# First group's q projected second and its attention begun then, with gate and compressed branch among its steps, in a hybrid retention and sparse-attention layer

## The chip, the core and the metric

The kernel runs on one core of a Trainium2 chip. The metric is device time in microseconds (us), as the median of several runs. The profile is one further execution, recorded by the hardware profiler; its span runs from the first to the last recorded instruction, and its own time is that of the same execution.

In what follows PE is TensorE's matmul, PEld its loading of weights, DVE is VectorE, ACT is ScalarE, POOL is GpSimd, and SP is SyncE, on whose queue all DMAs of this kernel are issued.

## What is computed

One layer on `x` of 512 tokens by 1024. After an RMSNorm, one projection gives everything: q, k, v and gate of a retention group (8 heads of 64), and q, gate, three pairs of k and v (compressed, selected, window; 2 kv heads of 64 each) and branch gates of a sparse-attention group. Cut to its core:

```python
h = rms_norm(x, norm_w)
rq, rk, rv, rg, nq, ng, ck, cv, sk, sv, wk, wv, gl = split(h @ w_in)
o_ret = rms_norm(retention(rq, rk, rv), ret_norm_w)        # rope on rq, rk; decay, causal
y_ret = o_ret * silu(rg)
q  = rms_norm(nq, q_norm_w)
kc = rms_norm(silu((blocks(ck) + pos_k) @ w1_k) @ w2_k, k_norm_cmp)   # blocks of 32, stride 16
vc = silu((blocks(cv) + pos_v) @ w1_v) @ w2_v
o_cmp, p_cmp = softmax_attention(q, kc, vc)
o_slc = attention over the blocks of 64 with the highest p_cmp, k = rms_norm(sk, k_norm_slc)
o_win = causal window attention, k = rms_norm(wk, k_norm_win)
y_nsa = (g0 * o_cmp + g1 * o_slc + g2 * o_win) * silu(ng)   # g = sigmoid(gl + b_gate)
out = x + concat(y_ret, y_nsa) @ w_out
```

In what the kernel's names say, NQ is the projection of the attention's q, NG of its gate, SK of selected and window k and v, CK of compressed k and v; a 0 or 1 behind them is the kv group (four query heads each). RQ, RK, RV, RG are the retention's.

## The kernel before, in words

Every product of two fp32 matrices is done as three products of fp32r halves: `wh` is the rounded copy of a weight tile, `wl` the rest, and likewise `hTh` and `hTl` for the activations; high by high, high by low and low by high are summed in PSUM. Weights come in units of 512 KB (`raw`, two buffers). ACT makes `wh` from a unit (two casts of 128x512), and `wl = raw - wh` is subtracted by DVE or by POOL; a string such as "VPVP" in `add_units` says which of them takes which unit's half, and some are left for the planner to choose (`either`).

There are two ways to project. `proj` keeps the activations in the array (128 tokens) and moves 256 columns of weights, so that the result has tokens on partitions; its instructions read `psacc<-wh,hTl` with 128x256. `proj_f` keeps the weights in the array and moves all 512 tokens, so that the result is transposed (columns on partitions); they read `psacc<-hTh,wh` with 128x512. Accumulation in PSUM uses the tag "acc" (3 banks), scores "S" (2), transposes "T" (2), outputs "O" (1).

The program is recorded in one order, stage by stage: NG0, CK, the gather of the compression's input (`compress_in`), SK and NQ0 are "drained" (recorded entirely), and then attention begins. Each step of an attention tile is a generator: `stage_a` makes scores (`psS`), the mask (DVE), row maximum (`mx`, DVE) and exponential (`P`, ACT); `stage_b` scales `P`, transposes it (four 128x128 `psT`), splits it in `PTh` (ACT) and `PTl` (DVE) and multiplies by v (`psO`). Between the steps `fill(FILL_A[g] * c)` takes so many ns of projection pieces from a list of "fillers". The retention's pairs of heads (`ret_pair`) run in the same way, with `FILL_R`; the result of a pair goes through a norm on DVE and POOL (`oS`, `ss`, `rs`, `yr`), and is transposed on PE (`y_transpose`, `psT<-identr,yr`) for the output product. That product is cut in `out1` (three of four units, plus the residual) and `out2` (the fourth unit).

The recorded operations are then ordered by a list scheduler (`arrange`): it has a table of costs by engine and shape, looks at the first 48 ready operations of each engine in the order of the record, and writes out the order of all five engines. `FIRST` moves three kinds of operations ahead in that order (weight halves, evacuations of "acc", loads of `raw`). So all instructions carry the line number of the loop that emits them, L1274, and are known by the names of their tiles. A queue of finished attention tiles (`pend`, with the tile `ot`) waits for the gate and is worked off by POOL (`fin_tile`).

Keys and queries are stored twice on partitions: `stack` copies a split tile `HL` into `B` with three DMAs of SP per half (64x512 and 64x1024).

Of the kernel before, what the change touches and what calls it, by code (L numbers as in the profile page):

```python
# [16 lines left out]
P = 128  # L17
T = 512
# [9 lines left out]
FILL_A = (1100.0, 1500.0)  # L28
FILL_R = (1200.0, 1500.0)
# [44 lines left out]
def footprint(ap):  # L74
# [4 lines left out]
    p0, base = divmod(int(ap.offset), row)  # L79
    starts, run = [base], 1  # L80
    for s, n in sorted(dims[1:], key=lambda d: abs(d[0])):
        if n == 1 or s == 0:
            continue
        if abs(s) <= max(run, 8):
            run += abs(s) * (n - 1)
        else:
            starts = [b + s * i for b in starts for i in range(n)]
# [4 lines left out]
    return ap.tensor.name, p0, p0 + dims[0][1], bits  # L92
# [253 lines left out]
def rope_tables():  # L346

    half = HD // 2
# [5 lines left out]
    tab = np.stack([np.concatenate([cos, cos, cos, cos], 0), np.concatenate([-sin, sin, -sin, sin], 0)], 1)  # L354
# [4 lines left out]
def layer_kernel(ctx: ExitStack, tc: tile.TileContext, x, xt, norm_w, w_in, w_out, ret_w, rowp, colp,  # L359
# [7 lines left out]
    SBB = {"B": 8, "P": 2, "raw": 2, "wh": 4, "wl": 4, "HL": 2, "qn": 2, "sq": 3, "oS": 1, "ot": 2, "kn": 2,  # L367
# [42 lines left out]
    wv = w_in.rearrange("(k p) c -> p k c", p=P)  # L410
    add_units(w_in, NG, (0, 1), "VPVP")
    add_units(w_in, CK, (0, 1), "VPVP")
    add_units(w_in, SK, (0, 1), "VPVP")
    add_units(w_in, NQ, (0, 1), "VVVP")
# [128 lines left out]
    w2t = S([P, 2, 2, 64], "w2t")  # L543
# [43 lines left out]
    def proj_f(evac):  # L587

        banks = [None, None]
        for u in range(4):  # L590
            wh, wl = next_unit()
            for c in range(2):
                if u == 0:
                    banks[c] = PS("acc")
                for kk in range(2):
                    k = 2 * u + kk
                    wc = slice(c * P, c * P + P)
                    mm(banks[c], wh[:, kk, wc], hTh[:, k], k == 0, False)
                    mm(banks[c], wh[:, kk, wc], hTl[:, k], False, False)
                    mm(banks[c], wl[:, kk, wc], hTh[:, k], False, k == KT - 1)  # L600
                if u == 3:
# [51 lines left out]

    ckv = S([P, NT, 256], "yr")

    def ck_evac(b, bank):
        for t in range(2):
            A.activation(ckv[:, 2 * b + t], bank[:, 256 * t:256 * t + 256], AF.Copy, scale=sc(rs1, 2 * b + t))
# [75 lines left out]

    kcT = S([P, 2, 64], "kcT", F32R)
# [5 lines left out]
    def compress_in(kv):  # L741
        tp = PS("T")
        for t in range(NT):
            PE.transpose(tp[:, t * 128:t * 128 + 128], ckv[:, t, kv * 128:kv * 128 + 128], ident)
        kv2 = S([P, 2, 256], "sq")
        tv = tp.rearrange("p (m r) -> p r m", r=2)
# [565 lines left out]
```

## Time and profile before

| what | value |
|---|---|
| runs | 340.67, 341.05, 341.1 us (median 341.05) |
| profiled execution, its own time | 340.4 us |
| its span | 338.6 us, so 1.8 us lie around it |
| granted TensorE clock over the span | 0.998 of full speed |
| PE busy | 329.6 us, 97% of the span, 2229 matmuls |
| PEld busy | 296.0 us, 87% |
| DVE, ACT, POOL busy | 248.5 (73%), 213.0 (63%), 124.3 us (37%) |

Busy time counts an engine from the start to the end of each instruction, and a matmul's modelled end overlaps the next one's start, so a row's mean duration of a matmul is longer than the spacing of matmuls in a run. The spacing is read from the chain of waits, where a run of matmuls stands as start, length and count.

### The profile page before, as it was taken

The page shows a single profiled execution, that of the slowest core. Times are in us where ns is not written, and L with a number is a line of the kernel's source. Part 1 is how long each engine was busy: PE and PEld are TensorE (multiplying, and loading weights), DVE is VectorE, ACT ScalarE, POOL GpSimd, SP SyncE. Part 2 cuts the span into 40 slices and gives each one's busy share as a digit, 9 for nine tenths or more (in the row PEclk, how much of TensorE's full clock was granted, in tenths as well). Part 3 has the DMA queues.
Part 4 walks back from the last instruction along what each step waited for, and adds up shares of the span by engine and source line. Part 5 has one row for each costly group of instructions (what it writes and reads, how often), then busy time and mean ns, then how long its engine had stood idle before and what let it go on. Part 6 is the DMA issues. An engine that isn't in the chain of part 4 may idle for free.

```text
span 338.6 us, 6267 instructions
## 1 busy us (share of the span) xinstructions
PE 329.6 (97%) x2229; PEld 296.0 (87%) x2229; DVE 248.5 (73%) x481; ACT 213.0 (63%) x474; POOL 124.3 (37%) x110
## 2 busy tenths in 40 slices
PE   8999999999999999999999999999999998999996
PEld 5988999978899787879999899787879997999995
DVE  2847667467878986668788978867777888786663
ACT  5874384355889878497885588778855553444210
POOL 1025206130232613468149535406184474130300
PEclk9999999999999999999999999999999999999999
DMA  7985562598434427331955612223635677021224
GB/s 235 390 289 162 133 179 68 156 216 234 146 116 128 124 62 180 107 95 34 255 143 157 150 36 64 63 62 96 155 101 149 153 204 234 2 94 33 95 73 175
DMA packets 40366, 46.96 MB, mean 139 GB/s; under 512 B 3984, under 2 KB 34320, under 8 KB 40336
## 3 DMA queue, kind: packets, MB, share of 16 engines
q1 hardware_dynamic: 40336, 46.58, 48.5%
q8 instruction: 17, 0.28, 0.3%
q14 instruction: 13, 0.11, 0.1%
HBM read 31.89 MB, written 2.10 MB: 100 GB/s over the span
## 4 chain that ended last, share of the span: by engine, by line
PE 73%; DVE 8%; DMA 7%; ACT 5%; issue 3%; POOL 2%; SPq 2%; DVEq 0%; ACTq 0%; POOLq 0%
PE psacc L1274 48%; PE psT L1274 9%; PE psS L1274 9%; PE psO L1274 6%; DMA B<-HL 4%; DVE wl L1274 2%; SPq L1274 2%; DMA xw<-qn 2%; ACT P L1274 2%; DMA B<-xt 1%; ACT wh L1274 1%; DVE mx L1274 1%; DVE sq L1274 1%; DVE psS L1274 1%; DVE PTl L1274 1%
## 5 line engine op out<-in xcount | busy, mean ns | idle before, releaser
L1274 PE MATMUL psacc<-wh,hTl 128*128 128x256 f32 x384 | 97.1, 284 | 0.0
L1274 ACT CAST wh<-raw 128x512 fp32r<-128x512 f32 x88 | 53.3, 622 | 42.3 <-PE psacc L1274 33.0
L1274 PE MATMUL psacc<-wl,hTh 128*128 128x256 f32 x256 | 73.5, 288 | 0.2 <-DVE wl L1274 0.2
L1274 PE MATMUL psacc<-wh,hTh 128*128 128x256 f32 x256 | 72.8, 286 | 0.0
L1274 PEld LDWEIGHTS psacc<-wh,hTl 128*128 128x128 f32 x384 | 68.5, 189 | 0.5
L1274 DVE TENSOR_TENSOR wl<-raw,wh 128x512 fp32r<-128x512 f32 x64 | 49.8, 788 | 19.3 <-ACT wh L1274 18.2
L1274 POOL TENSOR_TENSOR wl<-raw,wh 128x512 fp32r<-128x512 f32 x24 | 31.4, 1310 | 54.8 <-ACT wh L1274 36.1
L1274 PEld LDWEIGHTS psacc<-wl,hTh 128*128 128x128 f32 x256 | 48.4, 189 | 1.0 <-DVE wl L1274 0.4
L1274 PEld LDWEIGHTS psacc<-wh,hTh 128*128 128x128 f32 x256 | 48.1, 188 | 0.6 <-DVE sq L1274 0.2
L1274 PE MATMUL psS<-B,B 128*128 128x256 f32 (+3 forms) x176 | 42.5, 334 | 1.1 <-ACT P L1274 0.6
L1274 PE MATMUL psacc<-hTh,wh 128*128 128x512 f32 x96 | 39.0, 406 | 0.0
L1274 PE MATMUL psacc<-hTl,wh 128*128 128x512 f32 x96 | 38.6, 402 | 0.0
L1274 PE MATMUL psacc<-hTh,wl 128*128 128x512 f32 x96 | 38.4, 402 | 0.0
L1274 ACT ACTIVATE P<-psS,mx 128x128 f32<-128x128 f32 (+3 forms) x64 | 33.7, 531 | 3.6 <-DVE mx L1274 3.3
L1274 DVE TENSOR_TENSOR PTl<-psT,PTh 128x512 fp32r<-128x512 f32 x40 | 27.0, 687 | 9.4 <-ACT PTh L1274 9.1
L1274 PEld LDWEIGHTS psS<-B,B 128*128 128x128 f32 x176 | 28.1, 188 | 5.2 <-ACT P L1274 2.3
L1274 POOL TENSOR_TENSOR rs<-ss,mhalf 128x8 f32<-128x8 f32 (+2 forms) x14 | 17.9, 1282 | 36.9 <-DVE ss L1274 36.6
L1274 DVE TENSOR_TENSOR psS<-psS,cst 128x128 f32<-128x128 f32 (+2 forms) x68 | 23.1, 347 | 10.1 <-PE psS L1274 9.2
L1274 ACT CAST PTh<-psT 128x512 fp32r<-128x512 f32 x40 | 23.2, 589 | 9.7 <-PE psT L1274 9.0
L1274 DVE TENSOR_REDUCE mx<-psS 128x1 f32<-128x384 f32 (+3 forms) x44 | 28.2, 640 | 1.1
L1274 PE MATMUL psT<-identr,P 128*128 128x128 f32 x160 | 28.8, 275 | 0.1
L1274 ACT ACTIVATE P<-P,r 128x384 f32<-128x384 f32 (+3 forms) x53 | 26.5, 562 | 0.9 <-DVE r L1274 0.9
(187 smaller groups left out, 691.8 us busy)
## 6 DMA issues: line engine op xcount, KB each, us to landing
raw<-w_in SPq DMA_DIRECT2D x28, 512.0 KB, 3.7
B<-HL SPq DMA_DIRECT2D x56, 128.0 KB, 3.8
B<-HL SPq DMA_DIRECT2D x12, 256.0 KB, 4.4
B<-xt SPq DMA_DIRECT2D x8, 256.0 KB, 5.1
B<-x SPq DMA_DIRECT2D x4, 512.0 KB, 8.0
raw<-w1k SPq DMA_DIRECT2D x4, 512.0 KB, 4.8
raw<-w1v SPq DMA_DIRECT2D x4, 512.0 KB, 3.9
xw<-qn SPq DMA_DIRECT2D x32, 64.0 KB, 2.0
```

What stands on the lines that cost most here:

```text
L1274: fn(*args, **kw)
```

## The change

The order of the record becomes: NQ0, then SK, then attention of group 0 at once. NG0 and CK are no longer drained before it but are the first two fillers, ahead of the work that was the first filler before. CK, the output product (out1, out2 and the last piece) are projected by `proj_f`, 512 tokens wide, and the output is therefore written transposed (the residual is read from the transposed `xt`). The compressed k and v come out of CK's bank already transposed: one multiplication by a broadcast row of the norm's factors (`rsb`) puts them where the compression wants them, without the tile `ckv`, its four ACT evacuations, eight transposes on PE and the copies behind these. The columns of RQ and RK are interleaved on the host, so that swapping the rope's halves takes two DMAs of every second partition in place of four of 32 partitions. The tile `ot` has four buffers in place of two. Two factors of one half are moved from one scalar operation to another. The numbers in FILL_A, FILL_R and FIRST change.

In the listing of the program, PE's products 256 wide go from 1296 to 828, those 512 wide from 455 to 689, and those 128 wide from 268 to 260. POOL has 126 operations in place of 115, DVE 477 in place of 483, ACT 397 in place of 407, SP 178 in place of 195. Subtractions for `wl` are 33 on POOL and 55 on DVE, in place of 24 and 64.

```diff
-FILL_A = (1100.0, 1500.0)
-FILL_R = (1200.0, 1500.0)
+FILL_A = (1800.0, 1400.0)
+FILL_R = (1200.0, 400.0)
...
-    tab = np.stack([np.concatenate([cos, cos, cos, cos], 0), np.concatenate([-sin, sin, -sin, sin], 0)], 1)
+    tab = np.stack([np.stack([cos, cos], 1), np.stack([-sin, sin], 1)], 2).reshape(HD, 2, T)
+    tab = np.concatenate([tab, tab], 0)
...
-    SBB = {"B": 8, "P": 2, "raw": 2, "wh": 4, "wl": 4, "HL": 2, "qn": 2, "sq": 3, "oS": 1, "ot": 2, "kn": 2,
+    SBB = {"B": 8, "P": 2, "raw": 2, "wh": 4, "wl": 4, "HL": 2, "qn": 2, "sq": 3, "oS": 1, "ot": 4, "kn": 2,
...
+    add_units(w_in, NQ, (0, 1), "VVVP")
+    add_units(w_in, SK, (0, 1), "VPVP")
     add_units(w_in, NG, (0, 1), "VPVP")
     add_units(w_in, CK, (0, 1), "VPVP")
-    add_units(w_in, SK, (0, 1), "VPVP")
-    add_units(w_in, NQ, (0, 1), "VVVP")
...
-    w2t = S([P, 2, 2, 64], "w2t")
+    w2t = S([P, 2, 2, 64], "xw")
...
-    def proj_f(evac):
+    def part_f(o, c, u, wh, wl, lh, ll, first, last, ts=slice(0, T)):
+        for kk in range(2):
+            k = 2 * u + kk
+            wc = slice(c * P, c * P + P)
+            mm(o, wh[:, kk, wc], lh(k)[:, ts], first and kk == 0, False)
+            mm(o, wh[:, kk, wc], ll(k)[:, ts], False, False)
+            mm(o, wl[:, kk, wc], lh(k)[:, ts], False, last and kk == 1)
+
+    def proj_f(evac, lh=hh_, ll=hl_, us=(0, 1, 2, 3)):
 
         banks = [None, None]
-        for u in range(4):
+        for u in us:
             wh, wl = next_unit()
             for c in range(2):
-                if u == 0:
+                if u == us[0]:
                     banks[c] = PS("acc")
-                for kk in range(2):
-                    k = 2 * u + kk
-                    wc = slice(c * P, c * P + P)
-                    mm(banks[c], wh[:, kk, wc], hTh[:, k], k == 0, False)
-                    mm(banks[c], wh[:, kk, wc], hTl[:, k], False, False)
-                    mm(banks[c], wl[:, kk, wc], hTh[:, k], False, k == KT - 1)
-                if u == 3:
+                part_f(banks[c], c, u, wh, wl, lh, ll, u == us[0], u == us[-1])
+                if u == us[-1]:
                     evac(c, banks[c])
                 yield 1400
...
-    ckv = S([P, NT, 256], "yr")
-
-    def ck_evac(b, bank):
-        for t in range(2):
-            A.activation(ckv[:, 2 * b + t], bank[:, 256 * t:256 * t + 256], AF.Copy, scale=sc(rs1, 2 * b + t))
...
+    rsb = S([P, T], "rsb")
+    rbp = PS("T")
+    for i in range(NT):
+        PE.transpose(rbp[:, i * P:i * P + P], sc(rs1, i).to_broadcast([P, P]), ident)
+    A.copy(rsb, rbp)
...
-    def compress_in(kv):
-        tp = PS("T")
-        for t in range(NT):
-            PE.transpose(tp[:, t * 128:t * 128 + 128], ckv[:, t, kv * 128:kv * 128 + 128], ident)
+    def ck_evac(kv, bank):
+
         kv2 = S([P, 2, 256], "sq")
-        tv = tp.rearrange("p (m r) -> p r m", r=2)
+        bv, rv = (v.rearrange("p (m r) -> p r m", r=2) for v in (bank, rsb))
         for g in range(2):
             for r in range(2):
-                dst, src = kv2[r * 64:r * 64 + 64, g, :], tv[g * 64:g * 64 + 64, r, :]
-                if r == 0:
-                    A.copy(dst, src)
-                else:
-                    V.tensor_copy(dst, src)
+                rows = slice(64 * g, 64 * g + 64)
+                V.tensor_tensor(kv2[r * 64:r * 64 + 64, g, :], bv[rows, r, :], rv[rows, r, :], op=ALU.mult)
...
-            sqc = S([64, 64], "sqc")
+            sqc = S([64, 64], "sq")
...
-    V.tensor_scalar(gates, gates, 0.5, 0.5, op0=ALU.mult, op1=ALU.add)
+    V.tensor_scalar(gates, gates, 0.25, 0.25, op0=ALU.mult, op1=ALU.add)
...
-            A.activation(y, t, AF.Tanh)
+            A.activation(y, t, AF.Tanh, scale=0.5)
...
-            for a in range(4):
-                b = a ^ 1
-                SP.dma_start(xw[32 * a:32 * a + 32], xs_[32 * b:32 * b + 32])
+            for r in range(2):
+                SP.dma_start(xw[r:P:2], xs_[1 - r:P:2])
...
-            while len(pend) >= 2:
+            while len(pend) >= 4:
...
-    drain(proj_f(ng_evac(0)))
-    drain(proj(ck_evac))
-    drain(compress_inputs())
+    drain(proj(q_evac(0)))
     drain(proj(kv_evac(0)))
-    drain(proj(q_evac(0)))
-    fillers += [inter(proj_f(ng_evac(1)), cgen[0]), inter(proj(q_evac(1)), cgen[1]),
+    fillers += [proj_f(ng_evac(0)), proj_f(ck_evac), inter(proj_f(ng_evac(1)), cgen[0]), inter(proj(q_evac(1)), cgen[1]),
                 mark("q1"), cmp_attention(0), mark("g0"), proj_f(rope_evac(rkT, 0, 2)), proj_f(rope_evac(rqT, 0, 1))]
...
-    def out1_evac(c):
-        def go(b, bank):
+    def out1_evac(n):
+        def go(c, bank):
             if not part_sb:
-                part_sb.append(S([P, 2, 2, 1024], "hTh"))
-            dst = part_sb[0][:, b][:, :, 256 * c:256 * c + 256]
-            SP.dma_start(dst, xo[:, 2 * b:2 * b + 2, 256 * c:256 * c + 256])
-            V.tensor_tensor(dst, bank.rearrange("p (t c) -> p t c", t=2), dst, op=ALU.add)
+                part_sb.append(S([P, KT, T], "hTh"))
+            dst = part_sb[0][:, 2 * n + c]
+            SP.dma_start(dst, xo[2 * n + c])
+            V.tensor_tensor(dst, bank, dst, op=ALU.add)
         return go
 
-    def out2_evac(c):
-        def go(b, bank):
-            dst = part_sb[0][:, b][:, :, 256 * c:256 * c + 256]
-            V.tensor_tensor(dst, bank.rearrange("p (t c) -> p t c", t=2), dst, op=ALU.add)
-            SP.dma_start(oo[:, 2 * b:2 * b + 2, 256 * c:256 * c + 256], dst)
+    def out2_evac(n):
+        def go(c, bank, ts=slice(0, T)):
+            dst = part_sb[0][:, 2 * n + c, ts]
+            V.tensor_tensor(dst, bank, dst, op=ALU.add)
+            SP.dma_start(oo[2 * n + c][:, ts], dst)
...
-        fillers.append(proj(out1_evac(c), yh, yl, (0, 1, 2)))
+        fillers.append(proj_f(out1_evac(c), yh, yl, (0, 1, 2)))
...
-        drain(proj(out2_evac(c), yh, yl, (3,)))
+        drain(proj_f(out2_evac(c), yh, yl, (3,)))
     w = next_unit()
-    for i in range(NT):
-        bank = PS("acc")
-        part(bank, i // 2, (i % 2,), 3, *w, yh, yl, True, True)
-        dst = part_sb[0][:, i // 2, i % 2, 768:1024]
-        V.tensor_tensor(dst, bank[:, i % 2 * 256:i % 2 * 256 + 256], dst, op=ALU.add)
-        SP.dma_start(oo[:, i, 768:1024], dst)
+    for c in range(2):
+        for ts in ((slice(0, T),), (slice(0, 256), slice(256, T)))[c]:
+            bank = PS("acc")[:, :ts.stop - ts.start]
+            part_f(bank, c, 3, *w, yh, yl, True, True, ts)
+            out2_evac(3)(c, bank, ts)
...
-FIRST = (300, 300, 0)
+FIRST = (100, 300, 1000)
...
+    w = a(w_in)[0].copy()
+    for c0 in (RQ, RK):
+        w[:, c0:c0 + 512] = w[:, c0:c0 + 512].reshape(DM, 8, 2, 32).transpose(0, 1, 3, 2).reshape(DM, 512)
...
-    return r.results[0]["out"].reshape(1, T, DM)
+    return np.ascontiguousarray(r.results[0]["out"].reshape(DM, T).T).reshape(1, T, DM)
```

Where PE comes to the first scores of group 0. Before (psacc_240 is a product of the compression, psacc_222 a part of the next group's gate):

```order
L1274 MATMUL psacc_240<-wl_245,B_163 128x256
L1274 MATMUL psS_215<-B_102,B_104 128x256 x2
L1274 MATMUL psS_223<-B_102,B_104 128x256 x2
L1274 MATMUL psacc_240<-wh_244,B_163 128x256
L1274 MATMUL psacc_240<-wl_245,B_163 128x256
L1274 MATMUL psacc_222<-hTh_76,wh_247 128x512
L1274 MATMUL psacc_222<-hTl_77,wh_247 128x512
```

After (psacc_190 is NG0, the first filler, psacc_225 is CK, the second):

```order
L1261 MATMUL psacc_190<-hTl_77,wh_187 128x512
L1261 MATMUL psacc_190<-hTh_76,wl_188 128x512
L1261 MATMUL psacc_225<-hTh_76,wh_203 128x512
L1261 MATMUL psacc_225<-hTl_77,wh_203 128x512
L1261 MATMUL psS_182<-B_101,B_103 128x256 x4
L1261 MATMUL psS_191<-B_101,B_103 128x256 x4
L1261 MATMUL psacc_225<-hTh_76,wl_204 128x512
```

Ahead of the first score PE has 508 matmuls before and 369 after; between the first score of group 0 and the first of group 1 there are 440 before (170 of 256 columns, 166 of 512, 60 of 128, 28 of 64, 16 of 384) and 490 after (184, 202, 60, 28, 16). After, between the last product of SK and the first score stand 50 products 512 wide and four transposes.

On SP's queue, the copies of the selected and window keys (HL_188 before, HL_179 after). Before:

```order
L1274 DMA raw_217<-w1k 128x4x256
L1274 DMA raw_241<-w1k 128x4x256
L1274 DMA B_102<-HL_188 64x512
L1274 DMA B_103<-HL_188 64x512
L1274 DMA B_102<-HL_188 64x1024
L1274 DMA B_102<-HL_188 64x512
```

After:

```order
L1261 DMA raw_220<-w_in 128x4x256
L1261 DMA B_101<-HL_179 64x512
L1261 DMA raw_237<-w_in 128x4x256
L1261 DMA B_101<-HL_179 64x1024
L1261 DMA B_101<-HL_179 64x512
L1261 DMA B_102<-HL_179 64x1024
```

A load of a weight unit now stands between the first and the second of the copies.

Where PE transposes the result of the retention's first half for the output product, among the scores of its second half: two banks (psT_810 and psT_811 before, psT_807 and psT_808 after), in each first the two blocks of the first pair of heads, then the two of the second pair. The first pair's part of one bank stands higher up; psacc_859 and psacc_879 are pieces of out1. Before:

```order
L1274 MATMUL psacc_859<-wh_828,P_696 128x256
L1274 MATMUL psT_811<-identr_94,yr_570 128x128 x2
L1274 MATMUL psO_812<-PTh_831,B_799 128x384
L1274 MATMUL psT_810<-identr_94,yr_570 128x128 x2
L1274 MATMUL psT_811<-identr_94,yr_570 128x128 x2
L1274 MATMUL psO_812<-PTl_832,B_799 128x384
L1274 MATMUL psS_837<-B_736,B_714 128x256 x2
```

After:

```order
L1261 MATMUL psT_808<-identr_94,yr_565 128x128 x2
L1261 MATMUL psacc_879<-P_692,wl_852 128x512
L1261 MATMUL psacc_879<-P_692,wh_853 128x512
L1261 MATMUL psO_809<-PTl_823,B_803 128x384
L1261 MATMUL psS_827<-B_739,B_711 128x256 x2
L1261 MATMUL psS_827<-B_739,B_711 128x128 x2
L1261 MATMUL psacc_879<-P_693,wh_853 128x512
L1261 MATMUL psT_807<-identr_94,yr_565 128x128 x2
L1261 MATMUL psT_808<-identr_94,yr_565 128x128 x2
```

Three pieces of out1, each 512 wide, and the first scores psS_827 now stand ahead of the second pair's transposes. From the four transposes of the second pair's output (psT from oS, higher up) to these, PE has 30 products 256 wide, one of 512, five of 384 and four of 128 before, and 2, 22, 6 and 6 after.

## Rows read from the trace of the kernel before

**Rows 1.** Page, busy time, share of the span, instructions.

```profile
PE 329.6 (97%) x2229; PEld 296.0 (87%) x2229; DVE 248.5 (73%) x481; ACT 213.0 (63%) x474; POOL 124.3 (37%) x110
```

**Rows 2.** Chain of waits: start us, length us, what, matmuls in it.

```profile
19.10 9.33 PE psacc L1274 x40
...
44.45 14.16 PE psacc L1274 x119
...
75.73 0.23 issue
75.96 0.71 PE psS L1274 x4
...
137.32 1.28 PE psT L1274 x12
```

**Rows 3.** Stretches: length, busy time per engine, clock, DMA share, GB/s.

```profile
76.00:150.00 74.00, 72.91 (x435) 61.79 (x436) 58.64 (x126) 57.58 (x147) 25.87 (x21) 1.00 0.48 134
```

**Rows 4.** Waits of PEld, 76 to 151 us: total us, times, longest.

```profile
PEld psS L1274 <- ACT P L1274: 1.2, 3, 0.5
...
PEld psacc L1274 <- POOL wl L1274: 0.6, 1, 0.6
...
PEld psT L1274 <- DVE HL L1274: 0.4, 1, 0.4
```

**Rows 5.** Waits of all engines, 278 to 290 us.

```profile
PEld psT L1274 <- issue: 0.9, 1, 0.9
...
PE psT L1274 <- DVE qn L1274: 0.8, 1, 0.8
...
PEld psT L1274 <- DVE oS L1274: 0.2, 1, 0.2
```

**Rows 6.** Chain of waits, 276 to 290 us.

```profile
277.27 1.84 DVE wl L1274
279.14 0.69 DVE oS L1274
...
282.23 1.64 POOL rs L1274
...
285.97 1.28 POOL yr L1274
...
287.30 0.66 PE psT L1274 x4
```

**Rows 7.** Timeline of ACT, DVE and SP, 54 to 68 us: start, length.

```profile
55.41 0.38 ACT L1274 ACTIVATE sq<-psacc 128x256 f32<-128x256 f32 x1 [0.52 <-PE psacc L1274]
...
62.77 0.69 DVE L1274 TENSOR_TENSOR HL<-psT,HL 128x512 fp32r<-128x512 f32 x1
...
57.91 5.34 SPq L1274 DMA_DIRECT2D raw<-w1k  x2
63.34 4.52 SPq L1274 DMA_DIRECT2D B<-HL  x6
```

**Rows 8.** DMA issues: count, size, median us from issue to landing.

```profile
B<-HL SPq DMA_DIRECT2D x56, 128.0 KB, 3.8
...
xw<-qn SPq DMA_DIRECT2D x32, 64.0 KB, 2.0
```

**Rows 9.** Instructions of tile wl: ns min/median/max.

```profile
L1274 DVE TENSOR_TENSOR wl<-raw,wh x64: 674/693/1842, 15.0 to 324.6; 128x512 fp32r<-128x512 f32 x64
...
L1274 POOL TENSOR_TENSOR wl<-raw,wh x24: 1267/1290/1626, 23.3 to 295.1; 128x512 fp32r<-128x512 f32 x24
```

**Rows 10.** Page, costliest groups: busy us, mean ns of one, idle before.

```profile
L1274 DVE TENSOR_TENSOR wl<-raw,wh 128x512 fp32r<-128x512 f32 x64 | 49.8, 788 | 19.3 <-ACT wh L1274 18.2
...
L1274 DVE TENSOR_TENSOR PTl<-psT,PTh 128x512 fp32r<-128x512 f32 x40 | 27.0, 687 | 9.4 <-ACT PTh L1274 9.1
...
L1274 ACT CAST PTh<-psT 128x512 fp32r<-128x512 f32 x40 | 23.2, 589 | 9.7 <-PE psT L1274 9.0
```

**Rows 11.** Timeline of POOL, 276 to 279 us.

```profile
277.26 1.30 POOL L1274 TENSOR_TENSOR B<-sq,B 128x512 fp32r<-128x512 f32 x1
```

More of the change, by code (lines that the diff above doesn't have):

```diff
@@ L79, in footprint @@
     p0, base = divmod(int(ap.offset), row)
+    p1 = p0 + 1 + sum((n - 1) * (s // row) for s, n in dims if s and s % row == 0)
     starts, run = [base], 1
-    for s, n in sorted(dims[1:], key=lambda d: abs(d[0])):
+    for s, n in sorted((d for d in dims if d[0] % row), key=lambda d: abs(d[0])):
         if n == 1 or s == 0:
@@ L91, in footprint @@
         bits |= ((1 << (hi - lo + 1)) - 1) << lo
-    return ap.tensor.name, p0, p0 + dims[0][1], bits
+    return ap.tensor.name, p0, p1, bits
 def columns(ap):
@@ L803, in compress @@
             G.tensor_tensor(rsc, ssc, mhalf[:64, 0:1], op=ALU.pow)
-            kcn = S([64, 64], "kcn")
+            kcn = S([64, 64], "sq")
             V.scalar_tensor_tensor(kcn, kp[:64, :64], rsc, kwq[:64, 0], op0=ALU.mult, op1=ALU.mult)
@@ L841, in layer_kernel @@
     cgen = [compress(0), compress(1)]
-    def compress_inputs():
-        for kv in range(2):
-            compress_in(kv)
-            yield 100
     for i in range(NT):
@@ L911, in layer_kernel @@
     yn = S([P, 4, T], "yn")
-    rsb = S([P, T], "rsb")
-    rbp = PS("T")
-    for i in range(NT):
-        PE.transpose(rbp[:, i * P:i * P + P], sc(rsh, i).to_broadcast([P, P]), ident)
-    A.copy(rsb, rbp)
     def ng_evac(g):
@@ L1204, in yt @@
             yield 430
-    xo = x.rearrange("(t p) c -> p t c", p=P)
-    oo = out.rearrange("(t p) c -> p t c", p=P)
+    xo = xt.rearrange("(k p) t -> k p t", p=P)
+    oo = out.rearrange("(k p) t -> k p t", p=P)
     part_sb = []
@@ L1249, in layer_kernel @@
     for c in range(3):
-        drain(proj(out2_evac(c), yh, yl, (3,)))
+        drain(proj_f(out2_evac(c), yh, yl, (3,)))
     w = next_unit()
-    for i in range(NT):
-        bank = PS("acc")
-        part(bank, i // 2, (i % 2,), 3, *w, yh, yl, True, True)
-        dst = part_sb[0][:, i // 2, i % 2, 768:1024]
-        V.tensor_tensor(dst, bank[:, i % 2 * 256:i % 2 * 256 + 256], dst, op=ALU.add)
-        SP.dma_start(oo[:, i, 768:1024], dst)
+    for c in range(2):
[3 more added lines that the diff above has]
+            out2_evac(3)(c, bank, ts)
     prios = []
@@ L1292 @@
         "norm_w": np.ascontiguousarray(a(norm_w).reshape(KT, P).T),
-        "w_in": a(w_in)[0],
+        "w_in": w,
         "w_out": np.ascontiguousarray(np.concatenate([wo[1], wo[0]], 0)),
@@ L1306 @@
             for n, v in arrays.items()]
-    args.append(nc.dram_tensor("out", (T, DM), F32, kind="ExternalOutput").ap())
+    args.append(nc.dram_tensor("out", (DM, T), F32, kind="ExternalOutput").ap())
     with tile.TileContext(nc, schedule_with_timeline_sim=True) as tc:
```

## The prediction

> **What bounds the kernel now.** I read the page's busy times first: PE is busy for 97% of the span, its weight loads for 87%, and the next engine, DVE, for 73% [rows 1]. So the time is the number of matmuls times the spacing of each, plus stretches in which PE has nothing ready. The spacing comes from the chain of waits, in which long runs of products stand as one piece: 40 products of 512 columns in 9.33 us are 233 ns each, 119 of 256 columns in 14.16 us are 119 ns each, and a 128x128 transpose is 1.28/12 = 107 ns [rows 2]. Two narrow products cost 238 ns where one wide one costs 233.
>
> Busy time hides the stalls, because a modelled matmul overlaps the next: from 76 to 150 us, the attention of group 0, PE is shown busy for 72.91 of 74 us, at full clock [rows 3]. By spacing, the 440 matmuls of that stage are 170 x 0.119 + 166 x 0.233 + 60 x 0.107, about 65 us, and the 28 of 64 and 16 of 384 columns bring it to some 70 (their spacing put between those rows). About 5 us of its 75 are therefore lost. The waits of the weight loads there agree: nine kinds, of which three are shown, sum to 5.5 us, none above 1.2, spread over the links of the softmax chain [rows 4]. There is one more place of this kind, around 285 us, where PE and its weight loads waited in six rows for 3.1 us in all [rows 5]. The chain there is the norm of the retention's second pair: copy and add on DVE, the power on POOL for 1.64 us, the product with the gate on POOL for 1.28 us, and only at 287.30 the transposes [rows 6].
>
> **The change part by part.**
>
> Wide for narrow. CK, out1, out2 and the last piece give up 468 narrow products for 234 wide ones (12 of the last piece stay narrow): 468 x 0.119 = 55.7 against 234 x 0.233 = 54.5, so -1.2 us (0.9 to 1.6 as the runs' spacings vary by a nanosecond or two). All of it is on PE's path.
>
> The eight transposes of the compressed input go: 8 x 0.107 = -0.9 us.
>
> More cover at the output's transposes. From the transposes of the second pair's output to those of its normed result, PE has 30 narrow products, one wide, five of 384 and four transposes before, about 5.1 us, and after 22 wide, 2 narrow, 6 of 384 and 6 transposes, about 7.1 us (384 columns put at 175 ns, between the rows). Two more us of cover stand against a wait of 3.1; I take -1.5, and 0 to -3.1 as bounds.
>
> More work in group 0's stage. It has 490 matmuls in place of 440: 14 more narrow ones and 36 more wide ones, 14 x 0.119 + 36 x 0.233 = 10 us. They come from ahead of it, so the sum of work is as it was; what can fall is the 5.5 us of waits in the stage. As the stage's attention is the same and its filler grows from 70 to 80 us, each chain of softmax steps has about a seventh more to hide behind. Many of the waits are half a microsecond or less, which a filler or two more would cover, but they come from order too: a greedy order leaves such gaps with any filler. I take -1.7, a third; bounds 0 and -5.5.
>
> An earlier first score. Selected and window keys are now the last thing projected before the first score. Before, from the last square of that projection at 55.41 us to the split tile HL it was 7.4 us, then SP issued six copies in 4.52 us, 0.75 each [rows 7], and a copy lands 3.8 us after its issue [rows 8]. The first score needs the copies of its own group: the first three, with the raw load now between the first and second. From 55.41 the fourth issue is at 63.34 + 3 x 0.75 = 65.6, and lands at 69.4: 14.0 us. If the raw load waits for its buffer as the two before did, 5.34/2 = 2.67 us each [rows 7], it is 15.9. Behind the products of SK, PE has 50 wide products and four transposes, 12.1 us, as cover. So the first score can be late by 0 to 3.8 us, and the split of the selected keys would wait on SP behind a load of weights. In the kernel before, the first score followed q's own chain with PE idle for 0.23 us only [rows 2], so the planner had covered a chain of the same kind nearly to the end. I take +0.5, near that row. Should it be late, the gate's and CK's products stand on PE and run ahead of the score only as far as the written order allows, so the wait is whole.
>
> Edits that I cost at nothing: the rope's swaps, half the DMAs (32 of 2.0 us to landing, now 16 [rows 8]), are hidden under projection work, and the output's DMAs carry the same bytes. ACT loses four evacuations and DVE's evacuation of out1 is as large as before. More `ot` buffers only defer POOL's work on finished tiles. The factors of one half cost no instruction. If any of this was uncovered, it would cost one DMA's 2 us at the rope.
>
> Nine subtractions of `wl` go from DVE to POOL, where one takes 1290 ns in place of 693 [rows 9]. POOL is busy for 37% only [rows 1], and weights are made ahead, two raw and four split buffers deep, so I cost it at nothing in the sum. Here there is a row that speaks against it: at 277.27 us a subtraction on DVE took 1.84 us, and it began 10 ns after a POOL operation of 1.30 us [rows 6, 11], whose end is 0.55 us before its own, close to the usual 0.69. The average over all 64 is 788 ns against a median of 693, so what DVE lost to POOL is about 0.1 us each, 6 us over the span, off PE's path for most of it [rows 9, 10]. The Trainium skill, "SBUF — State Buffer", section "Who interferes with whom", says that a DVE instruction with two SBUF inputs contends with a GpSimd instruction that reads SBUF, and that the loser is fully blocked; the trace agrees in that one case. By that rule alone, each of POOL's eleven more operations could hold DVE for a whole operation, and the sum would be worse by what of that reaches PE. By the average of the rows they add about a microsecond to DVE, which has 90 to spare [rows 1].
>
> Sum: -1.2 - 0.9 - 1.5 - 1.7 + 0.5 = -4.8 on the span of 338.6, so 333.8; 1.8 us lie around the span, 335.6. The profiled execution's own 340.4 is 0.3 to 0.7 below the timed runs, so I add 0.4: **336.0 us**.
>
> **The rivals.**
>
> The waits only move. The stalls of group 0's stage and at the output's transposes come from order and appear elsewhere at the same size: -1.2 - 0.9 + 0.5 = -1.6, span 337.0, time 339.2. For it: nine kinds of wait, none large, as a greedy order leaves them. Against: 10 us of cover more, and the one at 285 us has a single chain. Chance 0.15.
>
> Both stalls vanish. -2.1 - 5.5 - 3.1 = -10.7, span 327.9, time 330.1. For it: the waits are short. Against: they are on tight links of the softmax chain. Chance 0.10.
>
> POOL's subtractions come late. Nine of them end 0.6 us later than on DVE; if PE waits for every one, 9 x 0.6 = 5.4 us, and the gain is gone: 341.4, which counts as no change. For it: the stage's waits before include one of 0.6 us for a subtraction of POOL's [rows 4]. Against: POOL makes 24 of them before, and this is the one that the stage shows. By the rule of "SBUF — State Buffer" in the Trainium skill the blocked subtractions on DVE would add to it. Chance 0.08.
>
> The retention's second half starves, which ends slower. FILL_R for it falls from 1500 to 400, so the record puts four times less of the output product among its twelve steps. A step's chain (scores, mask, PTh 0.59, PTl 0.69 [rows 10], product) is some 2 us of ACT and DVE in series. If the order follows the record, PE waits in each step. It decides from 4.8/12 = 0.4 us a step; at 0.9 us a step it is 11, at a likely 0.5 to 0.55 it is 6.3 and the time 342.3. Against: the planner takes the first ready among 48, and the excerpt shows pieces of out1 between those steps. Chance 0.11.
>
> **How the numbers follow.** My forecast has 0.56, with 332.5 to 338.5 as its own range (a third to two thirds of the 8.6 us of waits either way, and the first score). A difference of 0.2%, 0.7 us, is what a measurement here can tell. Faster: 0.56 + 0.15 + 0.10 = 0.81; same 0.08; slower 0.11. The range of 330.5 to 341.0 leaves out the slow case, the late subtractions and half of the vanishing stalls.
>
> **What would show it.** After: 2229 minus 234 minus 8 or so matmuls, 1987 with some records missing; 118 to 119 ns and 233 ns spacing as before; the wait of PE for the stacked keys at the first score near 65 us of a microsecond or less; weight-load waits in group 0's attention of 3.8 us in place of 5.5; the wait at the second pair's transposes 1.6 us in place of 3.1. Waits for PTh, PTl or the mask summing to over 5 us behind 290 us would show the slow rival; waits for `wl` from POOL of over 3 us, the other. A clock below full speed anywhere would make it all wrong.

## The result, and the profile after

The changed kernel takes 343.38 us (median of six runs, 341.99 to 346.07), the kernel before 340.86 in the same number: the ratio is 1.0069, 95% interval 1.0042 to 1.0096. It is slower by 0.7%, where 336.0 and faster was forecast. Two of its six runs stand at a mean granted clock of 1.0; they took 341.99 and 342.78 us, so the loss is not the clock's alone. The profiled execution has a span of 341.3 and an own time of 343.1 us, 2.7 above [rows 1]'s kernel in both, at the same mean clock of 0.998. Ratios, here and below, leave out runs that the chip disturbed, medians do not.

The page of the changed kernel, busy times and two groups of `wl`:

```profile
PE 327.3 (96%) x1987; PEld 281.8 (83%) x1987; DVE 242.9 (71%) x475; ACT 209.8 (61%) x464; POOL 138.7 (41%) x121
...
L1261 POOL TENSOR_TENSOR wl<-raw,wh 128x512 fp32r<-128x512 f32 x33 | 43.3, 1315 | 88.8 <-ACT wh L1261 71.2
...
L1261 DVE TENSOR_TENSOR wl<-raw,wh 128x512 fp32r<-128x512 f32 x55 | 44.7, 819 | 17.3 <-ACT wh L1261 17.0
```

PE has the 1987 matmuls that were forecast and is busy 2.3 us less, so the work did shrink; the span grew. The waits of PE over the whole run show where to look (total us, times, longest):

```profile
PE psT L1261 <- ACT PTh L1261: 1.9, 2, 1.5
PE psS L1261 <- DMA B<-HL: 1.6, 1, 1.6
PE psT L1261 <- DVE r L1261: 1.5, 1, 1.5
PE psT L1261 <- DVE oS L1261: 1.3, 1, 1.3
PE psO L1261 <- DVE oS L1261: 1.2, 1, 1.2
```

The last, 1.2 us at the start, was there before. The other four were not, or were small (0.4 us for PTh): a rope wait at 256 us, the first score at 56, a wait at 128, and one at 280 for the retention's output.

To add up small gaps as well, I take for each matmul its start less the sum of the usual spacings of all matmuls ahead of it (233, 176, 119, 107 and 108 ns for 512, 384, 256, 128 and 64 columns, 129 ns for the 96 of 280 columns near the start). The usual spacings sum to 317.8 us before and 315.8 after, the 2.0 us that the wide products and the missing transposes save. What is left is time lost on PE, by stage, in us (the run without loads ahead is e1 below):

| stage | before | changed | e1 |
|---|---|---|---|
| to the first score of group 0 | 5.3 | 6.1 | 4.9 |
| to the first score of group 1 | 4.9 | 4.7 | 5.1 |
| to the first product of out1 | 4.1 | 4.9 | 2.4 |
| to the last matmul | 2.9 | 5.8 | 5.2 |
| sum | 17.2 | 21.4 | 17.6 |

So -2.0 of work, +4.2 of gaps, and 0.5 between the last matmul's start and the span's end (3.6 before, 4.1 after) make the +2.7.

### The profile page after: what moved, and what is told of

Same layout as the page of the kernel before. It is cut to its first block, busy times and chain, and to the rows that moved or that the text cites. A ratio compares the mean times of both kernels' runs of the same rounds, so it can differ in the third digit from the quotient of the medians.

```text
span 341.3 us, 5750 instructions
## 1 busy us (share of the span) xinstructions
PE 327.3 (96%) x1987; PEld 281.8 (83%) x1987; DVE 242.9 (71%) x475; ACT 209.8 (61%) x464; POOL 138.7 (41%) x121
## 4 chain that ended last, share of the span: by engine, by line
PE 75%; DVE 8%; DMA 5%; issue 3%; ACT 3%; SPq 2%; POOL 2%; ACTq 0%; DVEq 0%; POOLq 0%
PE psacc L1261 50%; PE psS L1261 9%; PE psT L1261 9%; PE psO L1261 7%; DMA B<-HL 3%; SPq L1261 2%; DVE wl L1261 2%; DMA xw<-qn 1%; DVE HL L1261 1%; ACT P L1261 1%; DVE PTl L1261 1%; DMA nwc<-norm_w 1%; DVE qn L1261 1%; DVE ss L1261 1%; DVE sq L1261 1%
## 5 line engine op out<-in xcount | busy, mean ns | idle before, releaser
L1261 POOL TENSOR_TENSOR wl<-raw,wh 128x512 fp32r<-128x512 f32 x33 | 43.3, 1315 | 88.8 <-ACT wh L1261 71.2
L1261 PE MATMUL psacc<-hTl,wh 128*128 128x512 f32 (+1 forms) x180 | 65.9, 396 | 0.0
L1261 PE MATMUL psacc<-wh,hTh 128*128 128x256 f32 x224 | 63.9, 286 | 0.0
L1261 PE MATMUL psacc<-wl,hTh 128*128 128x256 f32 x224 | 63.9, 285 | 0.0
L1261 PE MATMUL psacc<-wh,hTl 128*128 128x256 f32 x224 | 63.9, 285 | 0.0
L1261 PE MATMUL psacc<-hTh,wl 128*128 128x512 f32 x112 | 44.7, 400 | 0.0
L1261 PEld LDWEIGHTS psacc<-wl,hTh 128*128 128x128 f32 x224 | 42.3, 189 | 0.6
L1261 PEld LDWEIGHTS psacc<-wh,hTl 128*128 128x128 f32 x224 | 42.2, 189 | 0.4
L1261 PEld LDWEIGHTS psacc<-hTl,wh 128*128 128x128 f32 x180 | 33.6, 188 | 6.4
L1261 ACT ACTIVATE P<-P,r 128x256 f32<-128x256 f32 (+3 forms) x51 | 25.0, 558 | 2.2 <-DVE r L1261 2.1
```

Of the source, the lines that this page charges most:

```text
L1261: fn(*args, **kw)
```

## The experiments

The first theory was that loads of `raw`, which the third number of FIRST moves 1000 places ahead, stand on SP in front of small copies. Rivals were that the new numbers of FILL_A or FILL_R starve the retention, or that the wide products cost more than they save.

**e1.** `-FIRST = (100, 300, 1000)` `+FIRST = (100, 300, 0)`

> The change with one number set back: loads of raw are no longer moved 1000 places ahead (third number of FIRST 0). SP then issues the copies of the selected keys without a load of raw between the first and second; the rest of PE's order is the same but for the place of the first scores. Theory late keys: the wait of 2.0 us of the weight load for B at the first score goes (0.3 us at most left), and the time falls by 1.3 to 2 us from the change's 343.4 to about 341.7. Theory starved end only: the first score's wait is made up later, time within 0.5 us of 343.4.

Measured 339.32, ratio 0.9949 (0.9933 to 0.9965): 4 us better than the change, and faster than the kernel before. SP's timeline around the first score (start, length), the changed kernel:

```profile
49.73 0.48 SPq L1261 DMA_DIRECT2D B<-HL  x1
51.20 0.37 SPq L1261 DMA_DIRECT2D raw<-w_in  x1
51.62 3.94 SPq L1261 DMA_DIRECT2D B<-HL  x5
```

The chain there, in the changed kernel:

```profile
50.48 0.70 DVE wl L1261
51.18 0.02 issue
51.20 0.37 SPq L1261
51.57 0.05 issue
51.62 5.58 DMA B<-HL
57.20 0.47 issue
57.67 1.19 PE psS L1261 x8
```

The load waits for its buffer, freed by `wl` at 51.18; only then come the other five copies, and one takes 5.58 us beside the 512 KB of the load. SP in e1:

```profile
50.14 4.84 SPq L1261 DMA_DIRECT2D B<-HL  x6
55.08 0.53 SPq L1261 DMA_DIRECT2D raw<-w_in  x1
```

Six copies without a break, and the weight load's wait at the score falls from 2.0 to 0.4 us. But that is 1.6 of 4 us, and the planner had written a new order for everything behind it.

**e2, e3.** FILL_A back, then FILL_R back, each alone: `-FILL_A = (1800.0, 1400.0)` `+FILL_A = (1100.0, 1500.0)`; `-FILL_R = (1200.0, 400.0)` `+FILL_R = (1200.0, 1500.0)`

> The change with FILL_A back at (1100, 1500). Theory starved first half: in the change the attention steps take up 1800 ns of projection pieces each, so that none are left for the second pair of heads in the retention's first half; with the old number the listing has 12.2 us of products between the two pairs' transposes where the change has 6.6, the stalls between 247 and 290 us fall from about 8.7 to about 4 us, and the time to 338.5 to 340, unless group 0's stage gives back one or two. Rival, starved second half (FILL_R[1] of 400): nothing changes there, 343.4 within 0.7.

> The change with FILL_R back at (1200, 1500). Theory starved second half: steps of the retention's second half get their pieces back and the time falls by 4 to 5 us, to about 339. Theory starved first half: the listing hardly differs (spacings of the transposes change by 1 us at most), the stalls between 247 and 290 us stay, time 343.4 within 0.7.

e2 took 349.17, ratio 1.0235 (1.0194 to 1.0276): against the theory. The last stage did lose less (4.8 in place of 5.8), but group 0's stage lost 8.1 in place of 4.7. e3 took 343.42, ratio 1.0081 (1.0050 to 1.0112), as the change: giving the second half its filler back gains nothing. My slow rival had a sign of its own, over 5 us of waits for PTh, PTl or the mask behind 290 us; in the changed kernel the weight loads wait 0.7 us there for PTh and PTl. It is not the cause.

**e4, e7.** The wide products in the old order, and the new order with the old products. e4 is the changed file with

```diff
-    drain(proj(q_evac(0)))
+    drain(proj_f(ng_evac(0)))
+    drain(proj_f(ck_evac))
     drain(proj(kv_evac(0)))
-    fillers += [proj_f(ng_evac(0)), proj_f(ck_evac), inter(
+    drain(proj(q_evac(0)))
+    fillers += [inter(
```

and the units and numbers of before; e7 is the reverse in the file of before.

> The change's wide products, direct evacuation of the compressed input, two rope DMAs and four ot buffers, but recorded in the order of the kernel before (gate, compressed branch, keys, then q) and with its numbers for FILL_A, FILL_R and FIRST. Theory that order and numbers made the loss: stalls as before and work less by 2.1 us, 338.5 to 339.3. Rival, the wide products or the evacuation behind them cost what they save (one bank of 512 columns to empty at once): 340.9 or more.

> The kernel before (narrow products, tile ckv and its transposes, four rope DMAs) recorded in the change's order, q, then keys, then attention, with gate, compressed branch and the gather of its input as fillers, and with the change's FILL_A and FILL_R; FIRST is (100, 300, 0), loads of raw not ahead. It has 2.1 us more of PE work than the run at 339.3. Theory that the order gains by more cover in group 0: 339 to 340. Theory that the order gains nothing and the wide products all: 341.0 to 341.7. If the products' saving is lost in part elsewhere: below 340.

e4 took 351.88, ratio 1.0304 (1.0278 to 1.0330), e7 345.67, ratio 1.0127 (1.0100 to 1.0154). Both halves alone lose, though e1 has both and wins. Neither theory foresaw that. e4's work is the 315.8 of the change; it loses 12.7 us in group 0's stage and 9.4 in the last. Stretches of e4 (length, busy of PE, PEld, DVE, ACT, POOL, granted clock, DMA share, GB/s):

```profile
100.00:110.00 10.00, 10.00 (x76) 9.42 (x75) 8.50 (x18) 9.45 (x24) 0.78 (x1) 1.00 0.41 128
110.00:120.00 10.00, 5.38 (x25) 3.13 (x24) 8.76 (x22) 7.57 (x22) 4.03 (x5) 0.78 0.56 158
```

PE runs dry while the compressed keys go through DVE and ACT (its waits there are 1.7 and 1.1 us for `kch` and `kn`, and 1.8 for a `P`), and the granted clock falls in the same stretch. The 12.7 and 9.4 us hold time at the lower clock as well.

**e5, e9, e6.** Loads ahead only behind or only before the 1500th operation of the change, `early = FIRST[2] if i > 1500 else 0` and the reverse; and loads ahead in the kernel before, `FIRST = (300, 300, 1000)`.

> The change, but loads of raw are moved ahead only where they are recorded behind the 1500th operation, that is some way into the attention of group 0; the first scores get their keys as in the run in which no load is moved ahead (339.3). Theory two places, the first score and the rope of the retention, where SP stands behind a load of raw while copies of HL and xw wait: only the first is mended, 341.3 to 342.3. Rival, all of the loss starts at the first score: 339.3 within 0.7.

> The change, but loads of raw are moved ahead only where they are recorded before the 1500th operation; the rest of the program has them in the order of the record. The listing has the load between the copies of the selected keys, and from the rope on it is that of the run at 339.3. Theory that most of the loss comes late, at the rope, where SP stands: the first score waits about 2 us as in the change, of which group 0's stage gives some back, 339.3 to 341.0. Rival, the loss starts at the first score: 342.5 to 344.

> The kernel before with one number changed, the third of FIRST from 0 to 1000 (loads of raw ahead). Theory that the load in front of small copies costs by itself: slower by 1 to 4 us, 342 to 345, with SP waiting at a load of raw for its buffer while B from HL or xw stand behind it. Rival, the cost needs the new order, since in the listing of this one no load comes between the keys' copies and the first score: 341 within 0.7.

e5: 344.58, ratio 1.0096 (1.0069 to 1.0123). e9: 345.79, ratio 1.0114 (1.0064 to 1.0164). e6: 348.31, ratio 1.0213 (1.0185 to 1.0240), with the load between the copies of q and a wait of 1.5 us for B at the first score. Either half costs as much as the whole, so the times are no sum of places. But neither half is at the clock of e1 (0.995 to 1.0): e5's runs have mean clocks of 0.984 to 0.990, e9's of 0.976 to 0.995. One less the mean clock, times the span, is an estimate of the most that the lower level can have cost: 5.5 us in e5's profile (341.9 at 0.984), more than the 5.0 by which its span is longer than e1's, and 4.1 us in e9's (344.7 at 0.988). What each half costs at full clock is therefore not shown. e6 had the sign right and missed the size.

**e8, e10, e11, e12.** e8 has an aim, which its expectation gives: FILL_R `(1600.0, 400.0)` in e1. The other three change numbers that aim at nothing: FILL_A `(1150.0, 1500.0)` in before; FIRST `(280, 300, 0)` in before; FIRST `(130, 300, 0)` in e1.

> The change without loads ahead (339.3), and FILL_R's first number 1600 in place of 1200: in the listing 12.4 us of products then stand between the transposes of the two pairs of the retention's first half, in place of 6.6. Theory starved second pair: the waits of 1.3 us for oS and 0.8 us for yr at 275 and 284 us shrink below half a microsecond each, and the time falls by 1 to 2 us, 337.3 to 338.3. Rival, the waits only move: 339.3 within 0.7, or slower where the first pair is then short of cover.

> The kernel before with FILL_A's first number 1150 in place of 1100, no other edit; the planner writes another order from the first attention tile on. Theory that any new order costs, since each draws its own gaps and the one before was a lucky draw: slower by 1 to 8 us, 342 to 349. Rival, the losses in these runs belong to the edits: 341 within 0.7.

> The kernel before with FIRST (280, 300, 0) in place of (300, 300, 0): weight halves 20 places less ahead, no other edit; PE's listing differs from about the first quarter on. Theory that any new order draws its own gaps: slower by 1 to 8 us. Rival: 341 within 0.7.

> The run at 339.3 (the change without loads ahead) with FIRST (130, 300, 0) in place of (100, 300, 0), no other edit. Theory that any new order draws its own gaps, and that 339.3 was a lucky draw too: 340.5 to 347. Rival, the order of the record and the wide products settle the time: 339.3 within 0.7.

Ratios to the kernel before: e8 1.0028 (1.0008 to 1.0049), e10 1.0091 (1.0056 to 1.0126), e11 1.0041 (1.0016 to 1.0065), e12 1.0004 (0.9984 to 1.0025). All four are slower than the kernel that they start from, by 0.4 to 0.9% or 1.4 to 3.1 us (e8 and e12 by their ratio less e1's). In e8 the gap ahead of the transposes from oS went from 1.3 to 1.1 us only, and others came (the last stage loses 7.8 in place of 5.2). So an edit that aims at nothing costs 1.4 to 3.1 us, where the single terms that I had priced are 0.5 to 1.7. Part of it is the clock. All runs of e11 stand at 0.999 to 1.0, and its loss is gaps alone. e10's runs have 0.985 to 0.990, e12's 0.984 to 0.995; by the estimate above the lower level took up to 3.4 us of e10's profile and 1.7 of e12's.

**e13 to e16.** So I kept the order of the change and moved only loads on SP's queue, behind the copies that follow them:

```diff
     STAT["busy"], STAT["order"] = busy, order
+    for o in [v for v in order if v.eng == "SP" and v.call[1][0].tensor.name.startswith("raw_")]:
+        limit = min(order.index(v) for v in order if v.i in o.succs)
...
+        if to > here and o.call[1][0].tensor.name.split('_')[1] in ("177",):
+            order.insert(to, order.pop(here))
```

> The change with one instruction moved and nothing planned anew: on SP's queue the load of raw_237 goes behind the five copies of the selected and window keys that stand behind it; the listings of PE, DVE, ACT and POOL are the same to the row. Theory load ahead: the weight load's wait of 2.0 us for B at the first score falls under 0.5, and the time by 1.5 to 2, to 341.4 to 341.9. Rival, the gap is given back by later waits of the same order: 343.4 within 0.7.

> The change with three loads of raw on SP's queue moved behind the copies of HL and xw that stand behind them, all in the retention's rope (raw_757, raw_788, raw_814); listings of the other engines the same to the row. Theory load ahead: of the stalls between 240 and 265 us, 4.6 us in the change against 1.7 in the run without loads ahead, 2 to 3 us go: 340.4 to 341.4. Rival: the copies are not what those steps wait for, 343.4 within 0.7.

> The change with the loads of the two runs before moved, and two more at the copies of the next group's q near 121 us (raw_439, raw_463); other listings the same. Theory load ahead at three places: the wait of 1.9 us at 127 us goes too, and the time falls by 4 to 5 us, to 338.5 to 339.5, as without loads ahead. Rival: less than 2 us, since what is gained at one place is waited for at the next.

> The change with every load of raw that stands in front of small copies moved behind them, 14 places, where the first use of the load comes later in the record; other listings the same. Theory load ahead: at least as good as the six moves, 337.5 to 339.5. Rival: a load issued late makes weights late, PE waits for wh and wl of which the change has almost none: 340 or more.

e13: ratio 1.0072 (1.0044 to 1.0100). The wait at the first score is gone from its waits and its profiled span is 339.6, the forecast 1.7 less, but the runs don't show it (the last section has the reason as far as it is known). e14: 1.0322 (1.0294 to 1.0351), e15: 1.0243 (1.0206 to 1.0280), e16: 1.0629 (1.0600 to 1.0658). The theory falls for the rope: a load issued later costs more there. ACT's timeline in e14:

```profile
247.09 0.59 ACT L1272 CAST PTh<-psS 128x512 fp32r<-128x512 f32 x1 [0.19 <-DVE psS L1272]
251.80 0.62 ACT L1272 CAST wh<-raw 128x512 fp32r<-128x512 f32 x1 [4.13 <-DMA raw<-w_in]
252.32 0.47 ACT L1272 CAST PTh<-psS 128x384 fp32r<-128x384 f32 x1
```

ACT stands 4.13 us at `wh` for the late load, with the retention's PTh behind it, and PE waits 2.5 us for that PTh. Not all of e14's loss is such waits: its profile has a mean clock of 0.980 against the change's 0.998, by the estimate above up to 6.3 of the 8.0 us between their spans. A load that is late on SP blocks ACT's queue as surely as an early one blocks SP's.

**e17, e18.** Back to the change's own rope. DVE's timeline there, changed kernel:

```profile
243.45 1.68 DVE L1261 TENSOR_TENSOR P<-yn,P 128x512 fp32r<-128x512 f32 x1 [1.29 <-ACT P L1261]
245.05 1.78 DVE L1261 TENSOR_TENSOR wl<-raw,wh 128x512 fp32r<-128x512 f32 x1
...
246.97 1.55 DVE L1261 TENSOR_TENSOR HL<-sq,HL 128x512 fp32r<-128x512 f32 x1
```

POOL's, at the same time:

```profile
243.28 1.30 POOL L1261 TENSOR_TENSOR xw<-xw,tab 128x512 f32<-128x512 f32 x1 [0.52 <-DMA xw<-qn]
244.66 1.63 POOL L1261 TENSOR_TENSOR sq<-sq,xw 128x512 f32<-128x512 f32 x1
246.25 1.72 POOL L1261 TENSOR_TENSOR P<-yn,P 128x512 fp32r<-128x512 f32 x1
```

Three DVE operations in a row take 1.55 to 1.78 us where 0.69 is usual [rows 9], each beside one of POOL's. The Trainium skill, "SBUF — State Buffer", section "Who interferes with whom", says that the loser of such a pair is fully blocked; here the trace agrees: each of the three ends 0.54 or 0.55 us after the POOL operation beside it, and together they lose 2.9 us (5.01 less 3 x 0.69). In order, HL's copies, the rope's transfer, ACT's `qn` and the PTh behind it follow, and then PE. The chain to PE's wait at 256 us, changed kernel:

```profile
251.98 4.96 DMA xw<-qn
...
257.44 0.49 ACT PTh L1261
...
257.98 0.39 PE psT L1261
```

I moved the two subtractions `P` back some 10 us in the same order (e17), and then also the load of e13 (e18):

```diff
+    for o, behind in ((lo[2], "PTl_696_756"), (lo[3], "wl_701_761")):
+        to = next(n for n, v in enumerate(order) if v.eng == o.eng and v.call[1][0].tensor.name == behind)
+        order.insert(to, order.pop(order.index(o)))
```

> The change with two instructions moved and nothing planned anew: the two subtractions P from yn (low halves for the output product, used only from about 270 us on) that run at 243.5 us on DVE and 246.2 us on POOL go about 10 us later on their engines; PE, ACT and SP are the same to the row. Theory DVE held by POOL: in the change three DVE operations in a row there (P 1.68, wl 1.78, HL 1.55 us where 0.69 is usual) run beside POOL operations, and the copies, the rope's transfer, ACT's qn and PTh behind it are late by their 2.9 us; with the two moved, DVE's HL ends 2 to 3 us earlier, PE's wait of 1.5 us for PTh at 256 us falls under 0.5, and the time by 1.5 to 2.5, to 341 to 342. Rival, the transfer's 5.0 us is what counts: the wait stays, 343.4 within 0.7.

> The run before with the load of raw_237 on SP also moved behind the five copies of the keys, so that two places of the change are mended and no engine's order is otherwise new. Theory that the change's loss is a few such places: span 337.3 to 338.3 in a profile at full clock, time 339 to 340.2, level with the run without loads ahead. Rival, waits move on: 342.5 or more.

e17: 348.00, ratio 1.0196 (1.0143 to 1.0248), worse than the change. e18: median 343.67 of runs from 339.39 to 348.18, ratio 1.0023 (0.9987 to 1.0059). e18's profiled execution has the span that was forecast: 337.6, 3.7 less than the change's, at the same clock, and 18.0 us lost in place of 21.4. DVE's timeline in it:

```profile
242.95 1.65 DVE L1276 TENSOR_TENSOR wl<-raw,wh 128x512 fp32r<-128x512 f32 x1 [2.39 <-ACT wh L1276]
...
244.73 0.69 DVE L1276 TENSOR_TENSOR HL<-sq,HL 128x512 fp32r<-128x512 f32 x1
```

HL is at its usual 0.69, in e17 too. But PE's wait for that PTh does not follow it: 1.5 us in the change, 2.1 in e17 and 0.9 in e18, and 0.5 in e13, whose three DVE operations are as slow as the change's (1.55, 1.79 and 1.55 us). All four are at full clock there. What the wait goes with is the rope's transfer, 4.96 us in the change; in e17, e18 and e13, a line of each:

```profile
256.98 4.99 DMA xw<-qn
...
249.58 4.13 DMA xw<-qn
...
252.02 3.90 DMA xw<-qn
```

So the theory falls, and the rival in e17's expectation is borne out: the transfer's 5.0 us is what counts. Why the same transfer in the same order takes 3.9 to 5.0 us is not shown. Nor is it shown that the second edit gave e18 its span: e13, without it, comes to 337.9 if the 10 us at a clock of 0.83 behind its pause at 127 us are counted at full clock (339.6 less 1.7, an estimate). The ratios put e18 1.6 us below the change, but their intervals overlap, and e17 alone went the other way, so for the times this is inconclusive. e17's whole span, at a mean clock of 0.975, is not compared.

## Why the prediction was wrong, step by step

The two terms for shrinking waits failed, and so did the new order that I had priced at nothing. The work was right: -1.2 - 0.9 forecast, -2.0 by spacing, and the spacings held. Of the edits costed at nothing, POOL's subtractions stand (no wait of PE for one is among those of the changed kernel), and FILL_R's new number is worth nothing (e3). That "the rope's swaps ... are hidden under projection work" failed: the wait of 1.5 us at 256 us is behind their transfer. e7, with the old four copies in the new order, waits 1.6 us for a PTh behind the same kind of transfer, so the new copies are not needed for it.

"More work in group 0's stage ... I take -1.7" failed. With 10 us more of filler the stage loses 4.7 in place of 4.9 (5.1 in e1). The waits of the weight loads behind the first score sum to 4.7 us, where 3.8 was to be the sign; 1.9 of them are one wait at 127 us, for copies in flight, that was not there before. In e1 that one is 0.4, and the sum is 5.9. The rival "the waits only move" was right about it: a filler does not go where the gap is unless the order puts it there. Its 339.2 is also what e1 measured, 339.32, but partly by luck: against the kernel before, e1's stages lose -0.4, +0.2, -1.7 and +2.3 us.

"More cover at the output's transposes ... I take -1.5" failed with the wrong sign: the last stage loses 2.9 more (2.3 in e1). The wait that I had counted did shrink: at the second pair's transposes it is 0.6 and 1.0 us, the 1.6 that was named. What came in its place are 1.3 us for oS at 280 us and, by spacing, 1.7 us in five gaps of 0.2 to 0.4 ahead of `psO` and `psS` between 273 and 285 us. The two pairs of heads came closer, with 6.6 us of products between their transposes (psT from oS) in place of 13.7, counted in the listings by spacing. That this made the wait for oS is not shown: e8 has 12.4 us there and still a gap of 1.1. Why oS is late stays open. Chain of the changed kernel:

```profile
280.17 0.69 DVE oS L1261
...
284.92 1.66 POOL rs L1261
286.57 0.02 issue
286.60 1.27 DVE rs L1261
287.87 0.02 issue
287.90 0.70 DVE qn L1261
288.60 0.14 issue
288.73 0.41 PE psT L1261 x2
```

From oS to the transposes it is 8.6 us, 8.2 before [rows 6].

"An earlier first score ... +0.5" had the mechanism right and the value too low: the wait of the weight load is 2.0 us, PE's 1.6. The prediction's own rows gave more. A landing 14.0 us after the last square, against 12.1 us of cover, is 1.9 us late even if the load does not wait for its buffer, so the bounds were 1.9 to 3.8 and not 0 to 3.8. The 0.5 was taken instead from [rows 2]'s 0.23, a chain without a load between the copies.

The step that was missing: the third number of FIRST moves every load, and I followed it at one place; and the order was planned anew throughout, which I priced at nothing. The stage from group 1 to out1, in which I had no term, lost 0.8 more, with the rope's wait of 1.5 us. e10 to e12 show what an order that aims at nothing can cost, 1.4 to 3.1 us, the clock's part included; e1 against the change is the same kind of difference. Whether the loads ahead cost 4 us by themselves, or one order was merely better than another, stays open: with the order fixed, the loads' place costs at the first score and helps at the rope. The four buffers of `ot`, the direct evacuation of the compressed input and the rope's copies were never set back alone.

## What to carry to other kernels

Where a planner writes the order, first measure two or three edits that mean nothing: here they cost 0.4 to 0.9%, about as much as the terms argued over, and a tuned kernel's order is likely to be one of the better draws. Price the instructions that disappear, by their spacing, in full, and shrinking waits at next to nothing; even new work in the very place can leave the gap (e8). To test a place, move one instruction in the fixed order and compare profiles of equal clock, at the wait itself as well as by the span (e17); and ask of a load moved ahead or back which in-order queue it now holds up, SP's or that of the engine that casts it.

## What the runs showed of the hardware

Runs of one kernel differed most where their clocks did. The kernel before stays mostly within 339.6 to 342.8 with mean clocks of 0.994 to 1.0; e18 goes from 339.4 to 348.2 with 0.973 to 1.0. Gaps alone do not do it: e11, with more gaps than the kernel before (20.9 us against 17.2), has 0.999 to 1.0 and stays within 342.6 to 344.0. One place can be followed: at 127 us PE waits for HL, whose buffer is held by copies in flight. The chain in the changed kernel:

```profile
123.58 4.95 DMA B<-HL
...
128.62 0.38 ACT HL L1261
...
129.03 0.42 DVE HL L1261
...
129.59 0.31 PE psT L1261 x2
```

All engines' orders up to there are the same in the change, e14 and e17, yet the weight load's wait is 1.9, 1.9 and 3.1 us. Two stretches of the changed kernel:

```profile
120.00:130.00 10.00, 8.54 (x49) 6.96 (x49) 7.32 (x16) 5.93 (x13) 4.77 (x4) 1.00 0.98 234
130.00:140.00 10.00, 10.00 (x52) 8.32 (x53) 7.58 (x16) 5.68 (x12) 6.32 (x6) 1.00 0.44 109
```

And of e9, where the wait is 3.6:

```profile
120.00:130.00 10.00, 7.85 (x44) 6.43 (x43) 6.39 (x12) 4.71 (x9) 4.47 (x4) 1.00 1.01 230
130.00:140.00 10.00, 8.94 (x34) 7.74 (x35) 3.95 (x10) 4.38 (x10) 2.13 (x2) 0.66 0.47 111
```

The DMA engines are busy throughout the first stretch in both. Behind the pause the granted clock stays at 1.00 in the change and is 0.66 in e9, that is, much of the stretch is at the lower of the two levels (1.2 and 2.4 GHz), and PE does 34 matmuls in place of 52. e13 had a wait of only 1.7 us and 0.83 behind it, e18 one of 2.0 and 1.00, so the pause's length alone does not settle it. A pause whose size hangs on transfers costs more than itself in some executions, and this blurs the medians of e13, e17 and e18.
